# Four weight tiles worked through in halves at the start of a two-layer encoder trunk

## The chip, the core and the metric

The kernel runs on one NeuronCore of a Trainium2 chip. Time is what the device takes for one execution, in microseconds. Lower is better. Five engines have queues of their own that run in order: TensorE (PE, matmuls), VectorE (DVE), ScalarE (ACT), GpSimd (POOL) and SyncE (SP), which here issues every DMA. A semaphore ties one queue to another wherever one reads what the other writes.

## The reference, cut to what matters

Two layers, each with an input projection of the normalised sequence, two head groups (RWKV-7 scans in both directions, and windowed attention with a sink), gates, and an output projection onto the residual. What the change touches is the first projection of layer 0:

```python
for l in range(DEPTH):                       # DEPTH = 2, x is (1, 256, 2048) f32
    h = rms_norm(x, norm_g[l])
    proj = jnp.einsum('btd,dc->btc', h, w_in[l])
    rw_in, g_rw, q, k_at, v_at, g_at = jnp.split(proj, col_splits, axis=-1)
    rw_in = bidir_token_shift(rw_in, shift_mu[l])
    r, k, v, xw, xa = jnp.split(rw_in, rw_splits, axis=-1)
    ...
    x = x + jnp.einsum('btc,cd->btd', mix, w_out[l])
return rms_norm(x, final_g)
```

## The kernel before

The sequence lies transposed: 2048 channels are 16 rows of 128 partitions, and each row holds 256 positions. `X0[:, k, :]` is row k of the input, `xT` its place in memory. A weight tile gives 128 output columns; it has 16 rows of 128 × 128 and is loaded as two pieces of 8 rows (512 KB each) into buffers `raw`, of which there are three.

Single precision is kept by splitting. ScalarE rounds a weight piece to `hi` (L241) and VectorE makes `lo`, the rest (L243), each in two instructions of 4 rows; the input is split the same way into `XH` (L203) and `XL` (L204). A row of a tile is then three matmuls into one accumulator `pm`: `hi` by XH (L311), `hi` by XL (L312), `lo` by XH (L313). There are two buffers of hi and two of lo.

The queue of rows is the class `Stream`. `S.run(n)` issues n rows ("steps"); the split of the next piece is put into the program two rows before the present one ends; `S.later(n, fn)` puts `fn` n rows further on. `gemm` appends a tile as two pieces of 8 rows and, behind the last, its evacuation `evac`. TensorE's order is the order of the code; the other engines' orders are set by a scheduler, within what the data allow.

The tiles of layer 0 begin with tile 0 (xw) and tile 1 (xa), then four for each of eight head pairs: k, v, r and a gate. The first row of a k tile also calls `ups` (L509), which loads two small pieces for the pair, `iup` (96 partitions) and `dup` (97 partitions), into `g`.

The norm is applied after the projection, so the matmuls need not wait for it. ScalarE squares the input in four instructions of 1024 columns and VectorE adds them (tile `mv`, L256). `Norm.add` sums over partitions on TensorE (`pr`, L217), VectorE and GpSimd make the inverse root, `Norm.spread` puts it on all partitions with four matmuls (`pr<-dg`, L227), and ScalarE copies it to `rb` (L229). Every evacuation multiplies `pm` by `rb` (`u`, L453), so none can begin before. Behind the k tile's evacuation stands a chain to `sl`, which the matmuls `pk` (L706) need.

At the start all 16 rows of x are split with one step of tile 0 behind each, and then:

```python
S.later(20, lambda: L0.norm.add([ACC[:, i * T : (i + 1) * T] for i in range(4)]))
S.later(27, lambda: L0.norm.spread())
S.run(8)
```

Of the kernel before, what the change touches and what calls it, by code (L numbers as in the profile page):

```python
# [9 lines left out]
F32 = mybir.dt.float32  # L10
# [85 lines left out]
C_KEEP = C_OFF["band"]  # L96
# [37 lines left out]
def hybrid_trunk_kernel(ctx, tc, xT, wi, wv, wo, par, fing, dup, iup, sink, pos, cst, out):  # L134
# [21 lines left out]
    def wbank(name):  # L156
        return wpair(name)[:, 0]
# [73 lines left out]
    def wload(src):  # L231
        raw = wrp.tile([128, 1024], F32, tag="raw", name="raw")
        SY.dma_start(out=raw, in_=src)
        return raw

    def wsplit(raw):
        hi = wsp.tile([128, 1024], F32R, tag="hi", name="hi")
        lo = wsp.tile([128, 1024], F32R, tag="lo", name="lo")
        for i in range(2):
            q = slice(i * 512, (i + 1) * 512)  # L240
            A.activation(hi[:, q], raw[:, q], AF.Copy)  # L241
            with tc.high_priority(offset=PRIO_LO):
                V.tensor_tensor(lo[:, q], raw[:, q], hi[:, q].bitcast(F32), op=ALU.subtract)  # L243
        return hi, lo

    def halves(src, raws=None):
        return [lambda i=i: wsplit(raws[i] if raws else wload(src[i])) for i in range(2)]

    class InTurn:

# [43 lines left out]

    S = Stream()

    def gemm(src, operands, evac, raws=None, begin=None, bank=None):

        box = []

        def step(kk):
            def f(w):
                if not box:
                    box.append(bank() if bank else ps_main.tile([128, T], F32, tag="m", name="pm"))
                    if begin:
# [5 lines left out]
                PE.matmul(pm, wh, rh[:, kk, :], start=(kk == 0), stop=False)  # L311
                PE.matmul(pm, wh, rl[:, kk, :], start=False, stop=False)  # L312
                PE.matmul(pm, wl, rh[:, kk, :], start=False, stop=(kk == 15))  # L313

            return f

        ld = halves(src, raws)
        S.add(ld[0], [step(k) for k in range(8)])
        S.add(ld[1], [step(k) for k in range(8, 16)], lambda: evac(box[0]))

    first_w = [wrp.tile([128, 1024], F32, tag="raw", name="raw") for _ in range(2)]
    G0 = cp.tile([128, NKT], F32, name="G0")
    X0 = Rows("s0", F32, "X0")
    SY.dma_start(out=first_w[0][:, 0:512], in_=wi[0, 0, 0, :, 0:512])
    SY.dma_start(out=G0, in_=par[0, :, P_NG : P_NG + NKT])
    for a, b in ((0, 2), (2, 4), (4, 8), (8, 12), (12, 16)):
        SY.dma_start(out=X0[:, a:b, :], in_=xT[:, a:b, :])
        if a == 0:
            SY.dma_start(out=first_w[0][:, 512:1024], in_=wi[0, 0, 0, :, 512:1024])
        if a == 4:  # L330
            SY.dma_start(out=first_w[1], in_=wi[0, 0, 1])
    mhalf = cp.tile([128, 4], F32, name="mhalf")
    V.memset(mhalf, -0.5)

# [106 lines left out]
    def queue_inputs(l):  # L441
# [4 lines left out]
        def inproj(ct, evac, **kw):  # L446
            gemm(wi[l, ct], lambda: (L.XH, L.XL), evac, **kw)
# [49 lines left out]

        if l == 0:

            inproj(0, lambda pm: S.later(29, lambda: xw_evac(pm)), raws=first_w, bank=lambda: wbank("pm")[:, 0:T])  # L500
            inproj(1, lambda pm: S.later(13, lambda: xa_evac(pm)))
        else:
            inproj(0, xw_evac)
            inproj(1, xa_evac)
# [27 lines left out]
            return evac  # L532

        for p, t in enumerate(L.ts):
            inproj(2 + 4 * p, shift_evac(p, new(t, "k", "kr", 4)), begin=ups(p, t))
            inproj(3 + 4 * p, value_evac(p, t))
            inproj(4 + 4 * p, shift_evac(16 + p, new(t, "r", "kr", 4)))
            inproj(5 + 4 * p, silu_evac(new(t, "gr", "vg", 8)))

# [744 lines left out]
```

## Time and profile before

| | |
|---|---|
| median of 3 runs | 1176.88 us (1175.71 to 1177.16) |
| the profiled execution | 1176.53 us, span 1174.8 us |
| TensorE busy | 1148.4 us, 98% of the span |
| VectorE, ScalarE busy | 907.0 us, 781.6 us |
| mean granted TensorE clock | 0.994 |
| moved by DMA | 166.63 MB |

Times in the views are microseconds from the start of the span. A row of a timeline has its start, its length, the engine, the line, the operation, output<-inputs, the shapes and the count; in brackets stands how long the engine had been idle before, and what ended that. In a table of windows a row has the stretch and its length, then the busy time of PE, PEld, DVE, ACT and POOL with the number of instructions, then TensorE's granted clock, the share of the 16 DMA engines that was busy, and GB/s. SPq is SyncE's queue of DMA issues; its rows show the issue, not the transfer. The chain of waits goes back from the last instruction, at each step to what released it.

### The profile page before, as it was taken

To read this page: it belongs to the slowest core of one execution; us is meant where nothing else is said; L and a number is where in the kernel's file an instruction comes from. 1 tells how busy PE (TensorE), PEld (TensorE's weight loads), DVE (VectorE), ACT (ScalarE), POOL (GpSimd) and SP (SyncE) were. 2 spreads that over 40 slices of the span, in tenths; PEclk is the share of its full clock that TensorE was granted. 3 is DMA by queue.
4 is the path that set the end of the run, shared out by engine and by line. 5 is a ranking of instruction groups with operands and counts; after the bars stand their busy time and mean duration, and the time that the engine had idled before them with its cause. 6 is when DMAs were issued, how large, how long until landed. Compare 5 with 4: busy or idle time off the path is not lost.

```text
span 1174.8 us, 38087 instructions
## 1 busy us (share of the span) xinstructions
PE 1148.4 (98%) x16151; PEld 1073.7 (91%) x16151; DVE 907.0 (77%) x2017; ACT 781.6 (67%) x1971; POOL 21.7 (2%) x23
## 2 busy tenths in 40 slices
PE   8999999999999999999999999999999999999996
PEld 6998999899899999899999889999999999899996
DVE  6899978888877677766678888978887767786654
ACT  6667867776875666645556677876786666675553
POOL 0000000000000000000000000000000000000000
PEclk8999999999999999999999999999999999999998
DMA  7544333333333443477655443333233344346653
GB/s 258 168 152 133 119 111 119 107 98 117 109 112 124 129 126 120 133 244 233 213 176 176 139 134 115 109 107 127 97 112 110 120 132 126 105 143 193 213 190 124
DMA packets 60410, 166.63 MB, mean 142 GB/s; under 512 B 7728, under 2 KB 22736, under 8 KB 60240
## 3 DMA queue, kind: packets, MB, share of 16 engines
q1 hardware_dynamic: 60240, 164.21, 43.4%
q8 instruction: 126, 2.06, 0.7%
q14 instruction: 44, 0.36, 0.1%
HBM read 157.37 MB, written 4.19 MB: 138 GB/s over the span
## 4 chain that ended last, share of the span: by engine, by line
PE 63%; DVE 15%; issue 14%; ACT 5%; DMA 2%; SPq 0%; POOL 0%; DVEq 0%; POOLq 0%; ACTq 0%
PE pm L311 15%; PE pm L313 13%; PE pm L312 13%; DVE lo L243 4%; PE pg L832 3%; PE pcc L995 2%; DVE kd L256 1%; ACT hi L241 1%; PE py L1007 1%; DVE th L256 1%; PE py L980 1%; PE pcc L1023 1%; PE pd L939 1%; DVE FR L256 1%; DVE mv L256 1%
## 5 line engine op out<-in xcount | busy, mean ns | idle before, releaser
L243 DVE TENSOR_TENSOR lo<-raw,hi 128x512 fp32r<-128x512 f32 x560 | 372.2, 687 | 112.9 <-ACT hi L241 107.3
L241 ACT ACTIVATE hi<-raw 128x512 fp32r<-128x512 f32 x560 | 329.6, 625 | 168.0 <-PE pm L312 95.2
L311 PE MATMUL pm<-XHa,hi 128*128 128x256 f32 x832 | 246.9, 297 | 1.9 <-ACT XHa L203 1.4
L311 PE MATMUL pm<-XHb,hi 128*128 128x256 f32 x832 | 243.2, 292 | 0.0
L313 PE MATMUL pm<-XHb,lo 128*128 128x256 f32 x832 | 233.8, 281 | 2.4 <-DVE lo L243 2.4
L313 PE MATMUL pm<-XHa,lo 128*128 128x256 f32 x832 | 234.2, 281 | 1.3 <-DVE lo L243 1.1
L312 PE MATMUL pm<-XLa,hi 128*128 128x256 f32 x832 | 234.3, 282 | 0.5 <-DVE XLa L204 0.3
L312 PE MATMUL pm<-XLb,hi 128*128 128x256 f32 x832 | 233.7, 281 | 0.0
L311 PEld LDWEIGHTS pm<-XHa,hi 128*128 128x128 f32 x832 | 157.0, 189 | 14.9 <-issue 3.2
L311 PEld LDWEIGHTS pm<-XHb,hi 128*128 128x128 f32 x832 | 157.0, 189 | 5.5
L313 PEld LDWEIGHTS pm<-XHb,lo 128*128 128x128 f32 x832 | 157.0, 189 | 3.2 <-DVE lo L243 3.2
L313 PEld LDWEIGHTS pm<-XHa,lo 128*128 128x128 f32 x832 | 157.3, 189 | 2.5 <-DVE lo L243 2.5
L312 PEld LDWEIGHTS pm<-XLa,hi 128*128 128x128 f32 x832 | 157.4, 189 | 1.1 <-DVE XLa L204 1.1
L312 PEld LDWEIGHTS pm<-XLb,hi 128*128 128x128 f32 x832 | 157.1, 189 | 0.3 <-DVE XLb L204 0.3
L1018 ACT ACTIVATE suv<-pcc 64x128 f32<-64x128 f32 x128 | 34.5, 270 | 72.3 <-PE pcc L1016 48.7
L311 PE MATMUL pm<-MHa,hi 128*128 128x256 f32 x256 | 72.0, 281 | 0.0
L313 PE MATMUL pm<-MHa,lo 128*128 128x256 f32 x256 | 71.9, 281 | 0.0
L312 PE MATMUL pm<-MLb,hi 128*128 128x256 f32 x256 | 71.8, 280 | 0.0
L311 PE MATMUL pm<-MHb,hi 128*128 128x256 f32 x256 | 71.7, 280 | 0.0
L313 PE MATMUL pm<-MHb,lo 128*128 128x256 f32 x256 | 71.7, 280 | 0.0
L312 PE MATMUL pm<-MLa,hi 128*128 128x256 f32 x256 | 71.7, 280 | 0.0
L311 PEld LDWEIGHTS pm<-MHa,hi 128*128 128x128 f32 x256 | 48.2, 188 | 0.8 <-issue 0.8
(292 smaller groups left out, 2317.3 us busy)
## 6 DMA issues: line engine op xcount, KB each, us to landing
raw<-wi SPq DMA_DIRECT2D x207, 512.0 KB
raw<-wo SPq DMA_DIRECT2D x64, 512.0 KB
raw<-wv SPq DMA_DIRECT2D x8, 512.0 KB
rrot<-u SPq DMA_DIRECT2D x80, 32.0 KB
vg<-xT SPq DMA_DIRECT2D x16, 128.0 KB
xd<-vg SPq DMA_DIRECT2D x16, 128.0 KB
vg<-xd SPq DMA_DIRECT2D x16, 128.0 KB
g<-dup SPq DMA_DIRECT2D x16, 97.0 KB
```

The costliest lines, as they stand in the source:

```text
L241: A.activation(hi[:, q], raw[:, q], AF.Copy)
L243: V.tensor_tensor(lo[:, q], raw[:, q], hi[:, q].bitcast(F32), op=ALU.subtract)
L256: return lambda *a, **k: tc.keep_in_program_order(getattr(self.engine, name)(*a, **k))
L311: PE.matmul(pm, wh, rh[:, kk, :], start=(kk == 0), stop=False)
L312: PE.matmul(pm, wh, rl[:, kk, :], start=False, stop=False)
L313: PE.matmul(pm, wl, rh[:, kk, :], start=False, stop=(kk == 15))
L832: PE.matmul(pg[:, h, c * 128 : (c + 1) * 128], BK[half[h], d, c, 1 - h : 3 - h, :].rearrange("p s j -> p (s j)"), MV[half[h], d, c].rearra ...
L939: PE.matmul(narrow(pd[:, d], h, c), hx(TT, d, c, h), sub(QF, h ^ d, d, c, d * b), start=True, stop=True)
L980: PE.matmul(py[half[h], c, :], GE[h][:, d, c, 1, :], SUV[:, d, c, h, :], start=(i == 0 and d == 0), stop=(i >= NC // 2), skip_group_check= ...
L995: PE.matmul(pc[half[h], 0, d, :], GE[h][r, d, ci[d], 0, :], SUV[r, d, ci[d], h, :], start=True, stop=True)
L1007: PE.matmul(py[half[h], ci[d], :], MV[half[h], d, ci[d], 1, :], SUV[half[h], d, ci[d], h, :], start=False, stop=False, skip_group_check=True,)
L1018: A.activation(here(h), pc[half[h], 1], AF.Copy)
```

## The change

The first four tiles (0, 1, 2 and 3) go into a list first. Their four first halves are put into the stream, in that order, then their second halves in the order 2, 0, 1, 3. The first loads are whole pieces of 512 KB: the first half of tile 0, x rows 0 to 3 and 4 to 7, the first halves of tiles 1 and 2, x rows 8 to 11. The rows 12 to 15 of x are loaded further down in the code, behind 27 steps. The accumulators of tiles 0 and 1 share one pair of banks, and the delays of the evacuations and of the norm have new numbers: `Norm.spread` came after 43 steps and comes after 53.

```diff
-    first_w = [wrp.tile([128, 1024], F32, tag="raw", name="raw") for _ in range(2)]
+    first_w = [wrp.tile([128, 1024], F32, tag="raw", name="raw") for _ in range(3)]
...
-    SY.dma_start(out=first_w[0][:, 0:512], in_=wi[0, 0, 0, :, 0:512])
+    SY.dma_start(out=first_w[0], in_=wi[0, 0, 0])
     SY.dma_start(out=G0, in_=par[0, :, P_NG : P_NG + NKT])
-    for a, b in ((0, 2), (2, 4), (4, 8), (8, 12), (12, 16)):
+    for a, b in ((0, 4), (4, 8), (8, 12)):
         SY.dma_start(out=X0[:, a:b, :], in_=xT[:, a:b, :])
-        if a == 0:
-            SY.dma_start(out=first_w[0][:, 512:1024], in_=wi[0, 0, 0, :, 512:1024])
         if a == 4:
-            SY.dma_start(out=first_w[1], in_=wi[0, 0, 1])
+            for i in (1, 2):
+                SY.dma_start(out=first_w[i], in_=wi[0, i, 0])
...
-            inproj(0, lambda pm: S.later(29, lambda: xw_evac(pm)), raws=first_w, bank=lambda: wbank("pm")[:, 0:T])
-            inproj(1, lambda pm: S.later(13, lambda: xa_evac(pm)))
+            inproj(0, lambda pm: S.later(7, lambda: xw_evac(pm)), raws=first_w[0:1], bank=bank_of(0), queue=lead)
+            inproj(1, xa_evac, raws=first_w[1:2], bank=bank_of(1), queue=lead)
...
+            ke = shift_evac(p, new(t, "k", "kr", 4))
+            if l == 0 and p == 0:
+                inproj(2, lambda pm, ke=ke: S.later(14, lambda: ke(pm)), raws=first_w[2:3], begin=ups(p, t), queue=lead)
+                inproj(3, value_evac(p, t), queue=lead)
+                for x in [a for a, _ in lead] + [lead[i][1] for i in (2, 0, 1, 3)]:
+                    S.add(*x)
...
-    for k in range(NKT):
+    for k in range(8):
         x_split(L0.XH, L0.XL, X0[:, k, :], k, 0)
         S.run(1)
+    S.run(12)
+    for k in range(8, 12):
+        x_split(L0.XH, L0.XL, X0[:, k, :], k, 0)
+        S.run(1)
+    SY.dma_start(out=C, in_=cst[:, 0:C_KEEP])
+    setup_ = setup()
+    S.run(7)
+    SY.dma_start(out=X0[:, 12:16, :], in_=xT[:, 12:16, :])
+    SY.dma_start(out=PR, in_=par.rearrange("l p n -> p l n"))
+    for k in range(12, 16):
+        x_split(L0.XH, L0.XL, X0[:, k, :], k, 0)
...
-    S.later(20, lambda: L0.norm.add([ACC[:, i * T : (i + 1) * T] for i in range(4)]))
-    S.later(27, lambda: L0.norm.spread())
-    S.run(8)
-    SY.dma_start(out=C, in_=cst[:, 0:C_KEEP])
-    SY.dma_start(out=PR, in_=par.rearrange("l p n -> p l n"))
-    setup_ = setup()
+    S.later(15, lambda: L0.norm.add([ACC[:, i * T : (i + 1) * T] for i in range(4)]))
+    S.later(22, lambda: L0.norm.spread())
     next(setup_)
-    S.run(8)
+    S.run(1)
```

Three places in the engines' orders. The first is SP's queue of loads, before, from the last loads of x on; `raw_220` and `raw_266` are tile 1, `raw_317` is the first half of tile 2, `t1` is the positions, and `C`, `PR` and `cst` are constants:

```order
L327 DMA X0b_89<-xT 128x1024 x2
L233 DMA raw_220<-wi 128x1024
L233 DMA raw_266<-wi 128x1024
L1182 DMA C_84<-cst 128x642
L1183 DMA PR_83<-par 128x2x124
L349 DMA t1_282<-pos 128x256
L350 DMA FG_113<-fing 128x16
L351 DMA SK_114<-sink 128x32
L233 DMA raw_317<-wi 128x1024
L513 DMA g_335<-iup 96x2x128
L513 DMA g_337<-dup 97x2x128
L353 DMA mv_286<-cst 128x960
```

And after, from the third load of x on; `raw_246` is the first half of tile 3, `raw_282` the second half of tile 2, `raw_355` that of tile 0:

```order
L331 DMA X0b_90<-xT 128x1024
L527 DMA g_218<-iup 96x2x128
L527 DMA g_220<-dup 97x2x128
L233 DMA raw_246<-wi 128x1024
L1195 DMA C_84<-cst 128x642
L233 DMA raw_282<-wi 128x1024
L1198 DMA X0b_90<-xT 128x1024
L1199 DMA PR_83<-par 128x2x124
L352 DMA t1_314<-pos 128x256
L353 DMA FG_112<-fing 128x16
L354 DMA SK_113<-sink 128x32
L233 DMA raw_355<-wi 128x1024
```

`iup` and `dup` moved from behind the constants and tile 2 to the place behind x rows 8 to 11, and x rows 12 to 15 moved from ahead of them to the fourth place behind them.

The second is VectorE around the additions of the squares, before; `raw_266` is the second half of tile 1:

```order
L243 TENSOR_TENSOR lo_223<-raw_220,hi_222 128x512 x2
L256 TENSOR_TENSOR mv_236<-mv_236,mv_238 128x1024
L356 TENSOR_TENSOR DP_101<-PR_83 128x26
L359 TENSOR_SCALAR DP_101<-PR_83 128x8
L256 TENSOR_TENSOR mv_236<-mv_236,mv_241 128x1024
L243 TENSOR_TENSOR lo_269<-raw_266,hi_268 128x512 x2
L256 TENSOR_TENSOR mv_236<-mv_236,mv_244 128x1024
```

After, where `raw_355` is the second half of tile 0 and `raw_412` that of tile 1:

```order
L256 TENSOR_TENSOR mv_303<-mv_303,mv_305 128x1024
L256 TENSOR_TENSOR mv_303<-mv_303,mv_308 128x1024
L243 TENSOR_TENSOR lo_358<-raw_355,hi_357 128x512
L256 TENSOR_TENSOR mv_303<-mv_303,mv_311 128x1024
L243 TENSOR_TENSOR lo_358<-raw_355,hi_357 128x512
L243 TENSOR_TENSOR lo_415<-raw_412,hi_414 128x512 x2
```

The additions moved from the second half of tile 1 to the second half of tile 0, which is worked through third from last of the eight halves, and the last addition stands between the two `lo` of that piece.

The third is TensorE at the spread of the norm, before, in the second half of tile 2 (`pm_334`), 35 steps ahead of `pk`:

```order
L311 MATMUL pm_334<-XHb_132,hi_374 128x256
L312 MATMUL pm_334<-XLb_134,hi_374 128x256
L313 MATMUL pm_334<-XHb_132,lo_375 128x256
L227 MATMUL pr_351<-dg_353,C_84 128x128 x2
L311 MATMUL pm_334<-XHb_132,hi_374 128x256
```

After, in the second half of tile 1 (`hi_414`; `pm_142` is the pair of banks of tiles 0 and 1):

```order
L311 MATMUL pm_142<-XHb_131,hi_414 128x256
L312 MATMUL pm_142<-XLb_133,hi_414 128x256
L313 MATMUL pm_142<-XHb_131,lo_415 128x256
L227 MATMUL pr_397<-dg_399,C_84 128x128 x2
L311 MATMUL pm_142<-XHb_131,hi_414 128x256
```

`pk` kept its place behind 78 steps, so 25 steps now lie between the two.

More of the change, by code (lines that the diff above doesn't have):

```diff
@@ L246, in halves @@
     def halves(src, raws=None):
-        return [lambda i=i: wsplit(raws[i] if raws else wload(src[i])) for i in range(2)]
+        return [lambda i=i: wsplit(raws[i] if raws and i < len(raws) else wload(src[i])) for i in range(2)]
     class InTurn:
@@ L295, in hybrid_trunk_kernel, with gemm @@
     S = Stream()
-    def gemm(src, operands, evac, raws=None, begin=None, bank=None):
+    def gemm(src, operands, evac, raws=None, begin=None, bank=None, queue=None):
         box = []
@@ L317, in gemm @@
         ld = halves(src, raws)
-        S.add(ld[0], [step(k) for k in range(8)])
-        S.add(ld[1], [step(k) for k in range(8, 16)], lambda: evac(box[0]))
-    first_w = [wrp.tile([128, 1024], F32, tag="raw", name="raw") for _ in range(2)]
+        parts = (ld[0], [step(k) for k in range(8)]), (ld[1], [step(k) for k in range(8, 16)], lambda: evac(box[0]))
+        if queue is not None:
+            queue.append(parts)
+        else:
+            for x in parts:
+                S.add(*x)
+    first_w = [wrp.tile([128, 1024], F32, tag="raw", name="raw") for _ in range(3)]
     G0 = cp.tile([128, NKT], F32, name="G0")
     X0 = Rows("s0", F32, "X0")
-    SY.dma_start(out=first_w[0][:, 0:512], in_=wi[0, 0, 0, :, 0:512])
+    SY.dma_start(out=first_w[0], in_=wi[0, 0, 0])
     SY.dma_start(out=G0, in_=par[0, :, P_NG : P_NG + NKT])
-    for a, b in ((0, 2), (2, 4), (4, 8), (8, 12), (12, 16)):
+    for a, b in ((0, 4), (4, 8), (8, 12)):
         SY.dma_start(out=X0[:, a:b, :], in_=xT[:, a:b, :])
-        if a == 0:
-            SY.dma_start(out=first_w[0][:, 512:1024], in_=wi[0, 0, 0, :, 512:1024])
         if a == 4:
-            SY.dma_start(out=first_w[1], in_=wi[0, 0, 1])
+            for i in (1, 2):
+                SY.dma_start(out=first_w[i], in_=wi[0, i, 0])
     mhalf = cp.tile([128, 4], F32, name="mhalf")
@@ L498, in queue_inputs, with bank_of, bank @@
         if l == 0:
-            inproj(0, lambda pm: S.later(29, lambda: xw_evac(pm)), raws=first_w, bank=lambda: wbank("pm")[:, 0:T])
-            inproj(1, lambda pm: S.later(13, lambda: xa_evac(pm)))
+            lead = []
+            pair = []
+            def bank_of(i):
+                def bank():
+                    if not pair:
+                        pair.append(wpair("pm"))
+                    return pair[0][:, i, 0:T]
+                return bank
+            inproj(0, lambda pm: S.later(7, lambda: xw_evac(pm)), raws=first_w[0:1], bank=bank_of(0), queue=lead)
+            inproj(1, xa_evac, raws=first_w[1:2], bank=bank_of(1), queue=lead)
         else:
@@ L534, in queue_inputs @@
         for p, t in enumerate(L.ts):
-            inproj(2 + 4 * p, shift_evac(p, new(t, "k", "kr", 4)), begin=ups(p, t))
-            inproj(3 + 4 * p, value_evac(p, t))
+            ke = shift_evac(p, new(t, "k", "kr", 4))
[3 more added lines that the diff above has]
+                for x in [a for a, _ in lead] + [lead[i][1] for i in (2, 0, 1, 3)]:
+                    S.add(*x)
+            else:
+                inproj(2 + 4 * p, ke, begin=ups(p, t))
+                inproj(3 + 4 * p, value_evac(p, t))
             inproj(4 + 4 * p, shift_evac(16 + p, new(t, "r", "kr", 4)))
```

## The prediction

> **What bounds the kernel now.** I read the page first, for the engine that carries the span.
>
> ```profile
> span 1174.8 us, 38087 instructions
> ...
> PE 1148.4 (98%) x16151; PEld 1073.7 (91%) x16151; DVE 907.0 (77%) x2017; ACT 781.6 (67%) x1971; POOL 21.7 (2%) x23
> ...
> PE 63%; DVE 15%; issue 14%; ACT 5%; DMA 2%; SPq 0%; POOL 0%; DVEq 0%; POOLq 0%; ACTq 0%
> ```
>
> TensorE is idle for 26.4 us in all, so a change to the start can give a few us at most. The profiled execution took 1176.53 us, 1.7 more than its span and 0.35 under the median of 1176.88. What a measurement can tell from no change, 0.2%, is 2.35 us. Next come TensorE's timeline and its granted clock over the start.
>
> ```profile
> 6.64 0.38 PE L311 MATMUL pm<-XHa,hi 128*128 128x256 f32 x1 [0.57 <-ACT XHa L203]
> 22.47 0.38 PE L313 MATMUL pm<-XHb,lo 128*128 128x256 f32 x1 [1.22 <-DVE lo L243]
> 26.60 1.84 PE L217 MATMUL pr<-C,mv 128*128 128x1 f32 x16
> 28.30 0.36 PE L311 MATMUL pm<-XHa,hi 128*128 128x256 f32 x1
> 33.84 0.28 PE L311 MATMUL pm<-XHa,hi 128*128 128x256 f32 x1
> 39.47 0.28 PE L311 MATMUL pm<-XHa,hi 128*128 128x256 f32 x1
> ```
> ```profile
> 5.92:9.33 3.41, 2.22 (x11) 1.47 (x11) 2.36 (x5) 2.34 (x5) 0.00 (x0) 1.00 0.97 299
> 9.33:12.75 3.41, 2.63 (x11) 2.10 (x11) 1.83 (x5) 2.41 (x6) 0.00 (x0) 0.50 1.02 410
> 12.75:16.16 3.41, 3.41 (x16) 3.13 (x16) 3.41 (x8) 3.41 (x9) 0.00 (x0) 0.50 1.01 366
> 19.57:22.99 3.41, 2.20 (x18) 1.99 (x18) 3.41 (x7) 3.35 (x8) 0.00 (x0) 1.00 0.08 28
> ```
>
> I count in steps: one row of a weight tile, three matmuls. Tile 3 begins at 33.84 and tile 4, step 64, at 39.47, so a step takes 0.352 us. From step 64 on TensorE's order is the same in both programs; 39.47 is the mark to beat. The norm's sums (26.60 to 28.30) cost 1.7 us. In the second table the third pair is TensorE's busy time, and the column of 1.00 and 0.50 its clock: half speed from 9.33 to 16.16.
>
> **Where the transfers are.** The DMA queue of SP hands eight semaphores round, so each issue below waited for the transfer eight places ahead of it, and its start dates that landing.
>
> ```profile
> 10.34 0.34 SPq L349 DMA_DIRECT2D t<-pos  x1
> 11.58 0.33 SPq L350 DMA_DIRECT2D FG<-fing  x1
> 12.86 0.33 SPq L351 DMA_DIRECT2D SK<-sink  x1
> 14.46 0.33 SPq L233 DMA_DIRECT2D raw<-wi  x1
> 15.67 0.33 SPq L513 DMA_DIRECT2D g<-iup  x1
> 16.93 0.27 SPq L513 DMA_DIRECT2D g<-dup  x1
> ```
>
> They date X0[4:8], the second weight piece, X0[8:12], X0[12:16] and the two pieces behind: about 1.25 us per 512 KB, and 3,080 KB landed by 14.46. Then something odd:
>
> ```profile
> 20.90:23.10 2.20, 0.98 (x8) 0.78 (x8) 2.20 (x4) 2.13 (x6) 0.00 (x0) 1.00 0.07 22
> ```
> ```profile
> 27.19 0.96 DVE L365 CAST LV<-mv 128x1536 uint8<-128x1536 f32 x1 [1.11 <-DMA mv<-cst]
> ```
> ```profile
> 59.19 5.48 DMA raw<-wi
> ```
>
> For 2 us the 16 DMA engines move 22 GB/s at a share of 0.07, one engine of 16. What is under way is `dup`, the last load issued before (16.93): 97 KB, all on one engine. At 22 GB/s it streams for 4.5 us. What stands behind it on that engine is late: `cst`, issued at 21.84, was only there at 27.19, and in the chain of waits a later 512 KB piece behind the next `dup` takes 5.48 us.
>
> **The change, part by part.**
>
> *First pieces.* X0[0:4] and the whole first weight piece must land before the first matmul (1,032 KB, where 520 KB do now), so TensorE starts about 1.5 us later than 6.64, near 8. Rows 4 to 7 need 1,544 KB as before: 10.34. The clock falls as before, and by 16.16 TensorE has done about 12 steps in either program. Nothing gained or lost there.
>
> *`iup` and `dup` overtake.* They stood behind 5.2 MB; now they stand behind X0[8:12], 3.1 MB, and the loads of tile 3's first half, C, tile 2's second half, X0[12:16], PR and tile 0's second half stand behind them. Six pieces and G0 are ahead: 3,080 KB, 14.4 by the rows above. `iup` (96 KB) is spread: 0.2. `dup`: at least 4.5 by its rate; at most 6.1, since `cst` less its 480 KB (1.17) starts at 26.0 while the 1,205 KB from C to `iup` end no earlier than 16.93 + 2.9. I take 5.0, near the rate, as the small loads in that stretch are slow too. Then 512, 321, 512 and 512 KB: 4.5. X0[12:16] lands at 14.4 + 0.2 + 5.0 + 4.5 = 24.1 instead of 14.46.
>
> Tile 3's first half lands near 20.9, and TensorE wants it at 16.16 + 12 × 0.352 = 20.4: with hi and lo a stall of 1.5 to 2. It costs nothing in the end, since the next wait is longer.
>
> *The squares.* Their order on ScalarE and VectorE:
>
> ```profile
> 12.99 3.29 ACT L203 ACTIVATE XHb<-X0b,G 128x256 fp32r<-128x256 f32 x8
> 16.19 1.14 ACT L241 ACTIVATE hi<-raw 128x512 fp32r<-128x512 f32 x2
> 17.23 2.00 ACT L256 ACTIVATE mv<-X0a 128x1024 f32<-128x1024 f32 x2
> 20.07 0.62 ACT L241 ACTIVATE hi<-raw 128x512 fp32r<-128x512 f32 x1
> 20.59 1.05 ACT L256 ACTIVATE mv<-X0b 128x1024 f32<-128x1024 f32 x1
> ```
> ```profile
> 21.73 1.28 DVE L243 TENSOR_TENSOR lo<-raw,hi 128x512 fp32r<-128x512 f32 x2
> 22.93 1.22 DVE L256 TENSOR_TENSOR mv<-mv 128x1024 f32<-128x1024 f32 x1
> ```
>
> Four XHb take 3.29 / 2 = 1.65, so the first square starts at 25.8, 8.6 later than now (17.23). The same chain then gives the first lo of tile 0's second half at 21.73 + 8.6 = 30.3 and its matmul, the stalled one at 22.47, at 31.0. TensorE wanted it at step 40, near 27.9: idle 3 us. The third addition now stands between the two lo (1.2), so the second is done at 30.3 + 0.6 + 1.2 + 0.7 = 32.8, and 46 steps are done at 33.2. The sums take 1.7 (34.9), the 18 steps left 6.3, the spread of the norm (four matmuls) 0.4: step 64 at 41.6, against 39.47. **+2.2 us.** Tile 0's second half itself lands by 27.3 at the latest and is hidden by the squares with 1.3 to spare.
>
> *Norm later, first use where it was.* The spread moves from step 43 to step 53, the matmuls `pk` stay at step 78.
>
> ```profile
> 31.64 0.61 PE L227 MATMUL pr<-dg,C 128*128 128x128 f32 x4
> 32.00 0.36 PE L311 MATMUL pm<-XHb,hi 128*128 128x256 f32 x1
> 44.52 0.28 PE L706 MATMUL pk<-sl,BONES 128*128 128x256 f32 x1
> ```
> ```profile
> 32.85 0.74 DVE L453 TENSOR_TENSOR u<-pm,rb 128x256 f32<-128x256 f32 x2
> ...
> 42.16 0.42 DVE L256 TENSOR_TENSOR sl<-t,mf 128x256 fp32r<-128x256 f32 x1
> ```
>
> VectorE needs 9.7 us from u to sl (32.85 to 42.58) and is done 1.9 before `pk`. The new queue has one lo less and one shift more there: 9.5. With 0.7 from the spread to u that is 10.2 after it, and TensorE arrives after 25 steps, 8.9. **+1.2 us** (bounds: 0, if waits inside the 9.7 vanish, and 2).
>
> Behind that all queues agree again; the later stalls stay. Sum: +3.4 us, 1179.9 on the profiled execution, 1180.3 on the median.
>
> **The rivals.**
>
> *The first transfers run faster.* 256 KB landed by 3.33, 520 KB by 6.08, 1,544 KB by 10.34:
>
> ```profile
> 3.33 0.63 ACT L241 ACTIVATE hi<-raw 128x512 fp32r<-128x512 f32 x1 [1.32 <-DMA raw<-wi]
> 6.08 0.51 ACT L203 ACTIVATE XHa<-X0a,G 128x256 fp32r<-128x256 f32 x1 [2.12 <-DMA X0a<-xT]
> 10.34 0.91 ACT L203 ACTIVATE XHa<-X0a,G 128x256 fp32r<-128x256 f32 x2 [1.79 <-DMA X0a<-xT]
> ```
>
> At the later 1.25 per 512 KB the last two stretches would take 0.6 and 2.5, not 2.75 and 4.26: 3.9 earlier. If larger pieces bring that, all moves up by 3.9: -1.7 + 1.2 = -0.5, 1176.4. Against it: X0[4:8], a whole 512 KB piece, was slow too, so time rather than size seems to matter. 14%. The Trainium skill, DMA: Bandwidth & Descriptors, section Bandwidth, speaks for this case: it asks for batches of 1 MiB or more; no run here isolates the size.
>
> *`dup` holds nothing up.* Then X0[12:16] lands at 19.1 and TensorE runs from step 12 at 16.16 through 34 steps to 28.1, with sums, spread and 18 steps to 36.5: -2.9. With the wait at `pk` 1175.2 (14%). If VectorE also reaches sl in time, 1174.0, **faster** (13%). The point that decides is X0[12:16] landing before about 19.5; against it speaks the late `cst`.
>
> *The clock falls a second time.* At 9.33 it fell after a window 65% busy in which no idle stretch exceeded 0.6 us, at 22.99 it did not after one as busy. The wait of 3 us at step 40 leaves its windows about half busy. Half clock over one or two windows of 3.41 loses 1.5 or 3.0: 1181.8 to 1183.3, 12%. The Trainium skill, TensorE: Matmul & The Clock Gate, section Why this matters for your kernels, puts the danger at idle gaps over about 3 us; the fall at 9.33, with no such gap, shows this case can be touchier.
>
> *The change is not what it says.* Its code says all four first halves first, and TensorE's order follows it. But the fourth half and X0[12:16] are not among the first loads.
>
> **How the numbers follow.** The forecast has 47%: 1178.5 to 1182. About 39 of it and the 12 of the clock lie above 1179.2 (slower 0.51), 8 and the rivals at 1175.2 and 1176.4 within (same 0.36), 13 below 1174.5. The range reaches from 1174.0 to 1183.0; the forecast's own is 1178.5 to 1182.
>
> **What would show it.** Right: a stretch at 22 GB/s near 15 to 19, waits of TensorE on lo of 1.5 us or more near 21 and of 3 near 28, one on sl of about 1, tile 4 starting after 41. Wrong: X0[12:16] split before 20, tile 4 before 38, or no wait at `pk`.

## The result, and the profile after

The changed kernel takes 1180.77 us (median of 6 runs, 1179.04 to 1183.81) against 1176.26 us for the kernel before, measured beside it (1175.36 to 1177.16): a ratio of 1.0042, 95% interval 1.0027 to 1.0056. Measured again on another chip it was 1179.16 against 1176.90 us, ratio 1.0019 (1.0010 to 1.0027). It is slower, by 2.2 to 4.9 us as the two ratios give it. The profiled execution took 1180.64 us, the span 1178.9.

TensorE's timeline first: its first step, the waits, the sums, the spread, step 64 and `pk`.

```profile
9.52 0.58 PE L311 MATMUL pm<-XHa,hi 128*128 128x256 f32 x1 [3.42 <-ACT XHa L203]
...
26.98 0.38 PE L311 MATMUL pm<-XHb,hi 128*128 128x256 f32 x1 [1.06 <-ACT hi L241]
29.12 0.38 PE L313 MATMUL pm<-XHb,lo 128*128 128x256 f32 x1 [1.64 <-DVE lo L243]
31.45 1.84 PE L217 MATMUL pr<-C,mv 128*128 128x1 f32 x16
36.91 0.95 PE L227 MATMUL pr<-dg,C 128*128 128x128 f32 x4
39.13 0.39 PE L311 MATMUL pm<-XHb,hi 128*128 128x256 f32 x1 [0.91 <-DVE u L456]
42.80 0.28 PE L311 MATMUL pm<-XHa,hi 128*128 128x256 f32 x1
...
47.91 0.34 PE L727 MATMUL pk<-sl,BONES 128*128 128x256 f32 x1
```

The sums come at 31.45 (26.60 before), step 64 at 42.80 (39.47) and `pk` at 47.91 (44.52): 3.39 us late, and no wait stands at `pk`. VectorE shows how close that was: `sl` ends at 47.81, 0.1 before `pk` starts, and `u`, which needs the norm's `rb`, starts 5.5 us later than the 32.85 of before.

```profile
38.32 0.76 DVE L456 TENSOR_TENSOR u<-pm,rb 128x256 f32<-128x256 f32 x2 [1.08 <-ACT rb L229]
47.40 0.41 DVE L256 TENSOR_TENSOR sl<-t,mf 128x256 fp32r<-128x256 f32 x1
```

Next SyncE's queue. Each row is an issue; its length is how long SyncE was busy with it.

```profile
5.84 0.37 SPq L527 DMA_DIRECT2D g<-dup  x1
6.33 7.13 SPq L233 DMA_DIRECT2D raw<-wi  x1
13.51 0.43 SPq L1195 DMA_DIRECT2D C<-cst  x1
14.13 0.33 SPq L233 DMA_DIRECT2D raw<-wi  x1
14.50 0.43 SPq L1198 DMA_DIRECT2D X0b<-xT  x1
14.98 0.45 SPq L1199 DMA_DIRECT2D PR<-par  x1
```

The piece behind `dup` holds SyncE for 7.13 us, where such an issue otherwise takes 0.33. With so little issued, the 16 DMA engines, which move 406 GB/s from 10 to 11 us, move 89 from 12 to 13 and 44 from 13 to 14. X0[12:16], which stands behind 31 steps in the code (8, 12, 4 and 7; not 27, as said above), is issued at 14.50, and ScalarE and VectorE date its landing and that of PR by waiting for them, though not for long (0.42 and 0.80 us):

```profile
21.80 1.71 ACT L203 ACTIVATE XHb<-X0b,G 128x256 fp32r<-128x256 f32 x4 [0.42 <-DMA X0b<-xT]
23.42 1.99 ACT L256 ACTIVATE mv<-X0a 128x1024 f32<-128x1024 f32 x2
```
```profile
23.63 0.19 DVE L359 TENSOR_TENSOR DP<-PR 128x26 f32<-128x26 f32 x1 [0.80 <-DMA PR<-par]
```

Last the clock, in windows (after the busy times comes the clock, as 1.00 or 0.50):

```profile
27.39:30.80 3.41, 1.77 (x13) 1.47 (x12) 3.41 (x5) 2.40 (x4) 0.00 (x0) 1.00 0.37 106
30.80:34.22 3.42, 3.36 (x29) 3.36 (x30) 2.11 (x5) 0.19 (x1) 0.66 (x1) 1.00 0.73 222
34.22:37.63 3.41, 3.41 (x20) 3.41 (x18) 2.42 (x9) 0.96 (x2) 0.69 (x1) 0.50 0.36 133
300.46:303.87 3.41, 1.63 (x45) 1.29 (x43) 2.79 (x7) 3.35 (x12) 0.00 (x0) 1.00 0.44 136
303.87:307.28 3.41, 3.41 (x17) 3.41 (x17) 3.04 (x8) 3.40 (x9) 0.00 (x0) 0.50 0.07 23
```

It falls at 34.22. The window just ahead of that has TensorE busy for 3.36 us, about half of it with the norm's sums; the window with the waits is the one before. It falls again at 303.87, behind a TensorE wait of 1.78 us on ScalarE that the kernel before has too (1.76 us at 299.46, without a fall in its one profile; its other executions may have one). Read at the first `pk` of each head pair, the lag is 3.2 to 3.5 us until 261 us, 4.7 behind the fall at 304, and 4.1 to 4.2 at the end. So of the span's 4.1 us the start gave some 3.2, and a fall of the clock far from the change the rest.

### The profile page after: what moved, and what is told of

Read it like the earlier page. It is cut to its first block, busy times and chain, and to the rows that moved or that the text cites. A ratio compares the mean times of both kernels' runs of the same rounds, so it can differ in the third digit from the quotient of the medians.

```text
span 1178.9 us, 38079 instructions
## 1 busy us (share of the span) xinstructions
PE 1150.1 (98%) x16151; PEld 1076.4 (91%) x16151; DVE 906.9 (77%) x2017; ACT 781.3 (66%) x1971; POOL 22.3 (2%) x23
## 4 chain that ended last, share of the span: by engine, by line
PE 67%; DVE 15%; issue 14%; ACT 3%; DMA 1%; SPq 0%; POOL 0%; DVEq 0%; POOLq 0%; ACTq 0%
PE pm L311 17%; PE pm L313 14%; PE pm L312 14%; DVE lo L243 4%; PE pg L853 3%; PE pcc L1016 2%; PE py L1028 1%; DVE kd L256 1%; PE pcc L1044 1%; DVE th L256 1%; DVE mv L256 1%; PE py L1001 1%; PE pd L960 1%; PE pcc L1034 1%; PE pza L712 1%
```

## The experiments

Times below are medians, with the ratio to the kernel before on the same chip and its 95% interval; the ratio is taken from all the runs and need not be the quotient of the two medians. Of each kernel there is one profile, of the changed one there are two. The table gathers the marks of the start from the profiles; landings are those of the trace's completion records.

| kernel | first step | X0[8:12], X0[12:16] landed | sums | u | sl done | pk | ratio |
|---|---|---|---|---|---|---|---|
| before | 6.64 | 12.8, 14.4 | 26.60 | 32.85 | 42.58 | 44.52 | 1 |
| changed | 9.52 | 14.4, 21.8 | 31.45 | 38.32 | 47.81 | 47.91 | 1.0042 |
| changed, again | 8.43 | 13.2, 20.8 | 31.33 | 37.35 | 46.85 | 46.90 | 1.0019 |
| dup in two | 9.39 | 14.5, 19.6 | 32.10 | 37.81 | 47.29 | 47.39 | 1.0008 |
| later evacuation | 8.85 | 13.7, 20.9 | 31.49 | 37.20 | 46.65 | 46.70 | 1.0028 |
| both | 7.45 | 13.3, 18.5 | 28.51 | 34.22 | 43.66 | 43.71 | 1.0009 |
| before + overtaking | 6.75 | 12.5, 16.9 | 28.93 | 34.47 | 44.55 | 46.53 | 1.0021 |
| small first pieces | 6.05 | 13.1, 22.3 | 33.00 | 38.71 | 48.19 | 48.25 | 1.0046 |
| early squares | 9.18 | 13.7, 15.1 | 27.41 | 37.67 | 44.84 | 47.87 | 1.0025 |
| early squares, dup in two | 8.43 | 13.1, 14.9 | 27.76 | 37.01 | 44.20 | 47.33 | 1.0038 |
| fill | 9.05 | 13.5, 20.9 | 31.81 | 41.09 | 50.58 | 50.64 | 1.0026 |
| own bank | 8.23 | 12.9, 15.6 | 28.87 | 35.35 | 44.41 | 44.47 | 1.0023 |
| own bank, dup whole | 7.54 | 12.2, 14.8 | 27.44 | 33.94 | 43.01 | 43.07 | 1.0010 |
| dup behind | 9.09 | 13.5, 16.0 | 26.98 | 36.21 | 46.17 | 46.22 | 1.0030 |

### dup in two transfers

```diff
+                    if n == "du" and l == 0 and p == 0:
+                        for a, b in ((0, RANK), (RANK, rows)):
+                            SY.dma_start(out=t[n][a:b], in_=src[l, :, a:b, p * 128 : (p + 1) * 128].rearrange("d r c -> r d c"))
+                        continue
                     SY.dma_start(out=t[n][0:rows], in_=src[l, :, :, p * 128 : (p + 1) * 128].rearrange("d r c -> r d c"))
```

RANK is 96. 

> The changed kernel, with the first pair's 97 rows of dup loaded in two transfers, of 96 rows and of one row, so that the rows are no longer all on one DMA engine. Theory A (the late sums are the price of the overtaking: dup on one engine holds SyncE's issue of tile 3's piece for 7.13 us, and with it C, tile 2's second piece, X0[12:16] and PR): SyncE's issue behind dup takes under 1 us, X0[12:16] lands at 18 to 20 us in place of 21.8 and PR at 19 to 21 in place of 23.6, TensorE's 2.7 us of waits at step 40 shrink to under 1, step 64 starts 1.5 to 3 us sooner than 42.80, and the time is 1177.8 to 1179.5, 1 to 3 us under the changed kernel. Rival B (the order of the halves itself costs: two more split tiles, the squares' order on ScalarE and VectorE, the bank pair that tiles 0 and 1 share): the loads come sooner, but step 64 stays within 0.7 us of 42.80, and the time within 0.7 us of 1180.8. Rival C (the clock's second fall at 34 us does it): the time follows whether a window at half clock stands between 20 and 45 us, and not the loads: 1178.5 to 1179.3 without one, whatever the loads do.

1177.35 us, ratio 1.0008 (0.9999 to 1.0018). On time and loads theory A came true, on TensorE's waits rival B did: those at step 40 add up to 1.68 us, and step 64 starts at 42.28, only 0.52 sooner. The 96 rows landed at 15.1, 0.3 behind `iup` (whole: 16.7 in the changed kernel, 2.1 behind it). The piece behind is issued in 0.37, and the DMA engines move 311 and 326 GB/s in the two microseconds from 12 to 14. X0[12:16] is issued hardly sooner than the 14.50 of the changed kernel, since SyncE waits ahead of it until VectorE's `lo` frees a weight buffer:

```profile
14.38 0.43 SPq L1202 DMA_DIRECT2D X0b<-xT  x1
```

It lands 5.1 us after X0[8:12] where it took 7.3 and 7.6, because the pieces ahead of it had landed sooner. But the sums came no sooner: 22.7 us after TensorE's first step, against 21.9 and 22.9. ScalarE's timeline says why:

```profile
20.69 1.15 ACT L241 ACTIVATE hi<-raw 128x512 fp32r<-128x512 f32 x2 [0.91 <-PE pm L312]
21.75 1.70 ACT L203 ACTIVATE XHb<-X0b,G 128x256 fp32r<-128x256 f32 x4
```

X0[12:16] lay there from 19.6, but its splits stand behind a `hi` that waits until TensorE gives a buffer back. With the loads in time, that wait stands where the transfer stood. So the times fell by more than this profile can account for, and rival C is not excluded. The profiled run took 1179.08 us and has a fall of the clock at 28.59. It is one of four runs of 1179.08 to 1179.99 us with a mean granted clock of 0.992; the other seven have 0.995 to 0.997 and took 1176.45 to 1177.47.

The Trainium skill, DMA: Bandwidth & Descriptors, section Why a DMA increments its semaphore by 16 and not by 1, has a transfer run on the largest number of engines up to 16 that divides its row count, so 96 rows on 16 and 97, a prime number, on one. The runs agree, with 22 GB/s for 97 rows before and 0.3 us behind `iup` for 96.

### Tile 0's evacuation two steps later

```diff
-            inproj(0, lambda pm: S.later(7, lambda: xw_evac(pm)), ...
+            inproj(0, lambda pm: S.later(9, lambda: xw_evac(pm)), ...
```

> The changed kernel, with the evacuation of tile 0 (which needs the norm's row factors) put in two steps later in program order, behind the last step of tile 1, so that step 54's matmul doesn't wait until VectorE has read the bank pair that tiles 0 and 1 share (0.91 us at 39.13). Theory A (that wait only stands where the wait for the norm at pk would stand otherwise: VectorE takes 9.5 us from u to sl either way): the wait at 39.13 goes, step 64 starts 0.9 us sooner, and TensorE waits 0.9 us at pk instead; the time is within 0.4 us of the changed kernel. Rival B (the bank pair's wait is a loss of its own): 0.7 to 1.1 us under the changed kernel.

1179.57 us, ratio 1.0028 (1.0016 to 1.0040). The wait at the bank (0.91 us, and 1.29 in the second profile of the changed kernel) went and came back at `pk`, larger, as theory A had it. The time cannot tell the two apart, since the ratio lies between the two measurements of the changed kernel:

```profile
46.70 0.39 PE L727 MATMUL pk<-sl,BONES 128*128 128x256 f32 x1 [1.41 <-DVE sl L256]
```

### Both edits

> The changed kernel with both edits: dup of the first pair in two transfers, and tile 0's evacuation two steps later. Theory A: with the loads in time the sums end early, so that neither the bank pair nor pk holds TensorE for more than 0.5 us: 1177.0 to 1178.7, and against the kernel with dup's edit alone -0.9 to +0.2. Rival B (the halves cost of themselves): within 0.7 us of the changed kernel; rival C (what is left is the norm's chain on VectorE, 9.5 us from u to sl against ten steps of 3.5 us and the work between): as theory A in the loads, but with a wait at pk of 1 us or more and no difference from the kernel with dup's edit alone.

1177.88 us, ratio 1.0009 (1.0000 to 1.0018): no difference from dup's edit alone, as rival C had it, with

```profile
43.71 0.38 PE L731 MATMUL pk<-sl,BONES 128*128 128x256 f32 x1 [1.31 <-DVE sl L256]
```

Two kernels thus show one thing: in the changed order `pk` is set by VectorE's chain from `u` (9.4 to 9.5 us in both, as in the profiles of the changed kernel), and what TensorE saves ahead of it is given back there. The profile of this kernel has `pk` 0.8 us sooner than before, and is 2 us behind at the end: about 1.5 us were lost at a fall of the clock at 299, and some 1.4 more between 500 and 620 us, which no fall on record explains. TensorE's early start, at 7.45, is part of the early `pk`.

### The overtaking alone, in the kernel before

```diff
         SY.dma_start(out=X0[:, a:b, :], in_=xT[:, a:b, :])
+        if a == 8:
+            for n, src, rows in (("iu", iup, RANK), ("du", dup, RANK + 1)):
+                first_u[n] = st("g", [2, 128], bufs=2)
+                SY.dma_start(out=first_u[n][0:rows], in_=src[0, :, :, 0:128].rearrange("d r c -> r d c"))
```

> The kernel before, and of the change the overtaking alone: iup and dup of the first pair are issued behind X0[8:12] and ahead of tile 0's second half and all that follows. Theory A (dup on one engine holds SyncE for some 7 us and with it tile 0's second half or tile 1's first and X0[12:16]): TensorE, which has a row ready each 0.7 us, waits 2 to 5 us around steps 8 to 14, and the norm is late by as much: 2.5 to 5 us over before (1178.8 to 1181.3). Rival B (dup's overtaking is harmless, and the halves' order costs the 4.5 us): within 0.6 us of before, with X0[12:16] landing within 1.5 us of 14.46.

1179.45 us, ratio 1.0021 (1.0012 to 1.0030): 1.4 to 3.5 us, in theory A's place, near its lower end. (In this kernel tile 0's second half is issued ahead of X0[8:12], so it is not among the loads that `dup` holds up; X0[12:16] is the first of them.) SyncE's row and TensorE's, then the windows, in which a clock of 0.98 or 0.52 means that the window lies across the edge of a stretch at half clock:

```profile
6.12 6.32 SPq L328 DMA_DIRECT2D X0b<-xT  x1
```
```profile
17.47 0.38 PE L311 MATMUL pm<-XHb,hi 128*128 128x256 f32 x1 [2.13 <-ACT XHb L203]
```
```profile
15.88:19.29 3.41, 1.69 (x10) 1.49 (x11) 1.81 (x5) 2.38 (x6) 0.00 (x0) 0.98 1.01 392
19.29:22.70 3.41, 3.41 (x18) 3.41 (x18) 2.29 (x3) 3.41 (x5) 0.00 (x0) 0.52 0.83 288
```

Here nothing of the halves is in the kernel, so the overtaking has a price by itself: X0[12:16] at 16.9 in place of 14.4, a wait of 2.13 us, and a stretch at half clock behind it. Whether `dup` in two would take that price away in this order was not run.

### The changed kernel again, and the small first pieces

> The changed kernel itself, on the chip of the three kernels that are run with it. 1179.5 to 1181.5 us, 2.5 to 4.5 over before on this chip, if the first measurement holds here; its runs scatter over some 4 us. Theory: they scatter because X0[0:4] lands late by as much as 2 us and because the clock falls to one half for one more stretch of 3.4 us in some runs; then the slowest runs have the lowest mean clock.

1179.16 us (1177.37 to 1180.81), 2.3 over before: less than in the first measurement, and just under the expected 1179.5. The eight runs with a mean clock of 0.992 or 0.993 took 1178.60 to 1180.81 us, the three with 0.994 or 0.995 took 1177.37 to 1179.03, as the theory had it. The sums again came at 31.33, with waits at step 40 of 0.40 and 1.22 where the first profile had 1.06 and 1.64. The clock fell for one stretch at 28, none at 304. X0[12:16] landed at 20.8, while ScalarE was still at a `hi` that had waited for TensorE, so its splits did not wait for it:

```profile
20.20 1.15 ACT L241 ACTIVATE hi<-raw 128x512 fp32r<-128x512 f32 x2 [0.75 <-PE pm L312]
21.26 1.70 ACT L203 ACTIVATE XHb<-X0b,G 128x256 fp32r<-128x256 f32 x4
```

The small first pieces:

```diff
-    SY.dma_start(out=first_w[0], in_=wi[0, 0, 0])
+    SY.dma_start(out=first_w[0][:, 0:512], in_=wi[0, 0, 0, :, 0:512])
...
-    for a, b in ((0, 4), (4, 8), (8, 12)):
+    for a, b in ((0, 2), (2, 4), (4, 8), (8, 12)):
         SY.dma_start(out=X0[:, a:b, :], in_=xT[:, a:b, :])
+        if a == 0:
+            SY.dma_start(out=first_w[0][:, 512:1024], in_=wi[0, 0, 0, :, 512:1024])
```

> The changed kernel with the first pieces as they were before: tile 0's first half in two loads of 256 KB, and X0[0:4] in two of two rows. Theory A (the prediction's: TensorE starts 1.5 us or more sooner, but works through those steps at half clock or waits, so that the same step is reached at the time of the sums): TensorE's first step at 6.6 to 7.0 us in place of 9.5, and the time within 0.7 us of the changed kernel. Rival B (the larger pieces are a loss of their own, since TensorE starts 2.9 us later and never waits long enough afterwards to make it up): 1.5 to 2.9 us under the changed kernel.

1183.41 us, ratio 1.0046 (1.0031 to 1.0061): rival B fell, and theory A erred on the other side.

```profile
6.05 0.39 PE L311 MATMUL pm<-XHa,hi 128*128 128x256 f32 x1 [0.20 <-ACT XHa L203]
...
19.73 0.39 PE L311 MATMUL pm<-XHa,hi 128*128 128x256 f32 x1 [1.41 <-ACT hi L241]
...
28.11 0.39 PE L311 MATMUL pm<-XHb,hi 128*128 128x256 f32 x1 [1.87 <-ACT hi L241]
```

TensorE starts 2.4 us sooner than in the kernel beside it and is 1.7 later at step 40: two more transfers stand ahead of `dup`, the issue behind `dup` is held until 14.7 us (13.5 in the first profile), and X0[12:16] lands 1.5 later. An early first matmul buys nothing here, with `dup` whole. The runs fall into two groups, four from 1179.35 to 1180.46 us and five from 1183.41 to 1185.57 with a lower mean clock (0.992 to 0.994, and 0.987 to 0.991); the profile is of the first group.

### The norm's work moved forward

The squares go between the steps, one by one, the sums to step 35, the spread to 46, the evacuation to 51; X0[12:16] is issued behind X0[8:12]. Of two kernels the second has dup in two as well.

```diff
-    for a, b in ((0, 4), (4, 8), (8, 12)):
+    for a, b in ((0, 4), (4, 8), (8, 12), (12, 16)):
...
-    S.later(15, lambda: L0.norm.add([ACC[:, i * T : (i + 1) * T] for i in range(4)]))
-    S.later(22, lambda: L0.norm.spread())
+    S.later(8, lambda: L0.norm.add([ACC[:, i * T : (i + 1) * T] for i in range(4)]))
+    S.later(19, lambda: L0.norm.spread())
```

> The changed kernel with the norm's work moved forward and dup left whole: X0[12:16] issued right behind X0[8:12], the four squares put on ScalarE one by one between the splits of the weight halves, the sums at step 35, the spread at step 46, and tile 0's evacuation at step 51. Theory A (what makes TensorE wait 1.6 to 2.7 us at step 40 and 0.9 to 1.4 at the bank pair or at pk is the place of the squares and of the norm in the engines' program order: on ScalarE they stand behind splits that wait until TensorE gives a hi tile back, whatever the loads do): no wait over 0.5 us at step 40 nor at pk, and the time 2.5 to 4.5 us under the changed kernel, 1176 to 1178. Rival B (the held loads are the cause: raw pieces behind dup still land late): 0 to 1 us under the changed kernel, with a wait of 1 us or more on a weight half.

> The same early norm, and the first pair's dup in transfers of 96 rows and of one. Theory A: the two edits add up: dup's edit gave about 2 us where the sums came late, but with X0[12:16] ahead of it only the weight pieces are behind dup, and TensorE needs the first of them at step 24: 0 to 1 us under the kernel with the early norm alone, 1174.5 to 1177, and under before. Rival B (dup still holds back what TensorE waits for): 2 us or more under the kernel with the early norm alone. Rival C (another wait takes the place of those removed, on VectorE's chain from u to sl of 9.5 us): within 0.7 us of the kernel with dup's edit alone, 1177 to 1178.

1180.67 us, ratio 1.0025 (1.0015 to 1.0034), and 1181.97 us, 1.0038 (1.0026 to 1.0051): both expectations fell. The sums came 4 us sooner (27.4 and 27.8), yet `pk` only at 47.9 and 47.3, 3.0 and 3.1 us after `sl` was done: now TensorE was late itself. In the second kernel:

```profile
20.97 0.38 PE L311 MATMUL pm<-XHa,hi 128*128 128x256 f32 x1 [1.99 <-ACT hi L241]
22.66 0.58 PE L313 MATMUL pm<-XHa,lo 128*128 128x256 f32 x1 [1.19 <-DVE lo L243]
```

Tile 3's first half had landed behind X0[12:16], `iup`, `dup` and C (17.7 us; with `dup` whole 20.6), and its split stood behind the squares. There are two chains to `pk`, and I had moved one by holding up the other.

### Filling the wait at step 40

```diff
+    def fill():
+        L0.norm.ps = wpair("pr")
+        for _ in range(6):
+            PE.matmul(L0.norm.ps[:, 1, T : 2 * T], L0.XH[:, 0, 0:128], L0.XH[:, 0, :], start=True, stop=True)
+
+    S.later(9, fill)
     S.later(15, lambda: L0.norm.add(
```

> The changed kernel with six more 128x256 matmuls, whose result nobody reads, ahead of the first step of tile 0's second half, where TensorE waits for the half's hi and lo (0.40 and 1.22 us in the last profile of the changed kernel, 1.06 and 1.64 in the first). Theory A (the wait is what makes the clock fall a second time, for one stretch of 3.4 us at half, which costs 1.2 to 1.7 us): no granted clock of one half between 20 and 45 us, and 0.5 to 1.5 us under the changed kernel, so a ratio to before of about 1.001. Rival B (the clock falls for the 16 one-column matmuls or for the waits before): the fall stays and the time is within 0.4 us of the changed kernel. Rival C (what sets pk is VectorE's chain behind the norm, not TensorE): the fall goes, TensorE reaches pk sooner and waits there for sl, and the time is within 0.4 us.

1178.96 us, ratio 1.0026 (1.0011 to 1.0040): no gain, so theory A is not borne out, and the fall of the clock stayed, as rival B had it. The fill ran ahead of the first wait only; in the profile, the slowest run (1185.22), the wait for `lo` was 2.03 us, and then:

```profile
27.02:30.43 3.41, 1.38 (x11) 1.38 (x11) 3.31 (x5) 2.62 (x4) 0.00 (x0) 0.96 0.29 79
30.43:33.84 3.41, 3.41 (x19) 3.41 (x17) 1.51 (x3) 0.00 (x0) 0.00 (x0) 0.50 0.82 253
33.84:37.26 3.42, 3.42 (x17) 3.42 (x18) 1.41 (x4) 0.73 (x2) 1.34 (x1) 0.50 0.35 131
37.26:40.67 3.41, 3.41 (x19) 3.41 (x19) 1.90 (x7) 0.42 (x1) 0.00 (x0) 0.54 0.16 34
```

Three stretches at half clock, though TensorE never idles in them, and `pk` at 50.64, 2.7 and 3.7 later than in the two profiles of the changed kernel. The sums lie in this time (3.41 us in place of 1.84); whether their one-column matmuls count as work for the clock was not tried. That the changed kernel's clock fell at 34.22, right behind a window half filled by the sums, points the same way. It is the clearest case of how far two executions of nearly the same order can lie apart.

### Both chains moved

Tile 3's first half, X0[12:16], C and PR are issued right behind X0[8:12], dup in two behind them; the squares stand after steps 11, 15, 24 and 30, the sums at 45, the spread at 52; tile 0 has a bank of its own.

```diff
+        if k == 0:
+            late_w.append(wload(wi[0, 3, 0]))
+            SY.dma_start(out=X0[:, 12:16, :], in_=xT[:, 12:16, :])
+            SY.dma_start(out=C, in_=cst[:, 0:C_KEEP])
+            SY.dma_start(out=PR, in_=par.rearrange("l p n -> p l n"))
...
+            own = (lambda: ps_c.tile([128, 512], F32, tag="y", name="pm")[:, 0:T], lambda: wbank("pm")[:, 0:T])
```

> The changed kernel rearranged where the runs so far showed waits: tile 3's first half, X0[12:16], C and PR issued in that order right behind X0[8:12] and ahead of iup and dup (dup in two), the squares put on ScalarE after steps 11, 15, 24 and 30, the sums at step 45 and the spread at 52, tile 0 in a bank of its own and evacuated at step 52. Theory A (two chains end at pk, TensorE's own and the norm's through u and sl on VectorE, and only moving both moves pk): no wait over 0.6 us at steps 24, 32, 40 and at the bank, sums by 26.5, u by 31.5, pk at 40 to 42.5 us (44.52 before), and 1173 to 1175.5 us. Rival B (every order of the halves meets ScalarE's and VectorE's limit, since the splits of x and of four tiles and the squares all come in the first 25 us): a wait of 1 to 2 us at another half, pk at 44 or later, and 1176.5 to 1179.

> The same with dup in one transfer. Theory A (dup's price depends on what is issued behind it: here tile 2's second half, needed at step 32): that piece lands 1.5 to 3 us later, TensorE waits 0.5 to 2 us at step 32, and the time is 0.5 to 2 us over the kernel with dup in two. Rival B (dup's rows on one engine hold nothing up that TensorE waits for): within 0.4 us of it.

1179.69 us, ratio 1.0023 (1.0014 to 1.0032), and with dup whole 1178.65 us, 1.0010 (1.0001 to 1.0020). In the profiles `pk` came at 44.47 and 43.07, 0.05 and 1.45 us ahead of before, so the lateness at `pk` is gone, short of the 40 to 42.5 expected (waits of 0.8 to 1.2 us on a `lo` or a `hi` remain, rival B's picture). The end of both is 2.1 and 2.8 us behind before all the same: the clock fell at 301 and 302, and at 73 in the second, at about 1.5 us each time. On dup's price theory A fell: the piece behind it landed at 21.2 in place of 19.5, TensorE waited 0.81 us for it, and the time is no longer than with `dup` in two.

### dup behind everything

```diff
-                inproj(2, lambda pm, ke=ke: S.later(14, lambda: ke(pm)), raws=first_w[2:3], begin=ups(p, t), queue=lead)
+                inproj(2, lambda pm, ke=ke: S.later(14, lambda: ke(pm)), raws=first_w[2:3], queue=lead)
+                L.first_ups = ups(p, t)
...
+    S.later(9, L0.first_ups)
```

Besides, sums, spread and evacuation stand one or two steps earlier. 

> The rearranged kernel (early squares, tile 0 in its own bank) with iup and dup of the first pair, whole, issued at step 40, behind all weight pieces up to tile 0's second half, the sums at step 43, the spread at 50 and tile 0's evacuation at 51. Theory A (what the halves cost is the late norm and the pieces held by dup, and both go away here): X0[12:16] lands by 15.8 us, no wait over 0.6 us at steps 24, 32 and 40, sums by 26.5, u by 33, and pk at 41.5 to 43.5 us, 1 to 3 us under before's 44.52; the time is 1174 to 1176.5 where the clock doesn't fall a second time, some 1.6 us more where it does, so a median of 1175 to 1177.5 and a ratio to before of 0.9985 to 1.0005. Rival B (the halves are bound elsewhere, at the splits on ScalarE and VectorE): pk at 44 or later, 1178 to 1180, ratio 1.001 to 1.0025.

1180.95 us, ratio 1.0030 (1.0019 to 1.0041). Up to the sums things went nearly as theory A had it (X0[12:16] at 16.0 and the sums at 26.98, for 15.8 and 26.5; a wait of 0.78 at step 32), but `pk` came at 46.22, which is rival B's place, and the time is above both ranges. The rows of SyncE, ScalarE and TensorE:

```profile
23.00 0.34 SPq L520 DMA_DIRECT2D g<-dup  x1
23.38 5.24 SPq L233 DMA_DIRECT2D raw<-wi  x3
```
```profile
32.27 2.38 ACT L241 ACTIVATE hi<-raw 128x512 fp32r<-128x512 f32 x4 [7.48 <-DMA raw<-wi]
```
```profile
32.96 0.58 PE L311 MATMUL pm<-XHb,hi 128*128 128x256 f32 x1 [2.26 <-ACT hi L241]
```
```profile
32.87:36.28 3.41, 3.32 (x14) 3.10 (x15) 2.97 (x7) 2.09 (x5) 0.00 (x0) 0.51 0.37 112
```

The price of `dup` moved with it: the next weight half lands 8.8 us after its issue began, TensorE waits 2.26 us for it at step 48, and the clock falls. No version beat the kernel before.

## Why the prediction was right

The forecast was 1180.3 us, the ratio of 1.0042 gives 1181.8 on the median shown before it, and the second measurement 1179.1. Of the signs named for being right, tile 4 after 41 came (42.80 and 41.78), and the wait near 28 (2.70 us, and 1.62 in the second profile, of 3). The stall near 21 and the wait on `sl` did not come, the DMA engines were slow sooner and less (44 GB/s at 13 to 14 us), and a sign named for being wrong, no wait at `pk`, came true. So direction and size came out, and the path to them only in part.

*First pieces.* TensorE started at 9.52 and 8.43, 1.8 to 2.9 late where 1.5 was taken. That it costs nothing held with `dup` whole: the small pieces, with a start at 6.05, were no faster, but TensorE then waited 1.41 us at step 24 for the piece behind `dup`. Small pieces together with `dup` in two were not run. The small pieces also answer the rival of faster first transfers: in pieces of 256 KB X0[0:4] was there by 7.5 us, in one of 512 KB by 7.8 in the kernel beside it, and by 6.8 to 8.9 in all profiles. The Trainium skill (DMA: Bandwidth & Descriptors, section Bandwidth) asks for batches of 1 MiB or more; no run here has one, and the step from 256 to 512 KB brought nothing.

*`iup` and `dup` overtake.* The loads came late as forecast, but by less, and little hung on it. `dup` was done 2.1 us after `iup`, not 5.0; what let it overlap with the loads ahead wasn't tried. That SyncE itself would be held was not foreseen. X0[12:16] landed at 21.8 and 20.8, not 24.1, and tile 3's first half at 17.8 and 17.4, not 20.9, so TensorE had no stall there. In the first profile ScalarE waited 0.42 us for X0[12:16] and VectorE 0.80 for PR; in the second neither waited, and its waits at step 40 (1.62 us) are those of the kernel with `dup` in two (1.68). So the late loads, on which the forecast rested, account for about 1.1 us in one profile and for nothing in the other.

*The squares.* The first square started at 23.42 and 22.86 (25.8 forecast), and 46 steps were done at 31.45 and 31.33 (33.2). The idle at step 40 was 2.70 us in the first profile and 1.62 in the second, forecast 3. What was missed is that ScalarE's order alone keeps some 1.6 us there: the splits and squares stand behind a `hi` that waits for TensorE, and the waits are 1.68 and 1.55 us in the two kernels whose loads came sooner. The kernel before has as much:

```profile
30.71 0.38 PE L313 MATMUL pm<-XHb,lo 128*128 128x256 f32 x1 [0.52 <-DVE lo L243]
```

This wait and the 1.22 us at 22.47 make 1.74.

*From there to step 64.* Forecast 8.4 us, measured 11.35 and 10.45. The bank pair took 0.91 and 1.29, which the forecast lacked, and the half clock about 1.5 by estimate (in the changed kernel's profile matmuls follow each other in 0.118 us at full clock and in 0.213 in the stretch from 34.22, where the first profile lost it; the second lost it at 28, ahead of the sums). The clock's second fall was a rival at 12%; it happened in both profiles. Against the kernel before, step 64 is 3.33 and 2.31 us late. Of this about 1.5 is the clock's, 0.9 and 1.3 the bank's, and +1.0 and -0.1 the waits at step 40 over the 1.74 of before; 0.7 goes off, since step 16 came sooner (17.31 and 17.27, against 17.98), and 0.6 and 0.4 stay unexplained. So the +2.2 that the squares were to cost is not what happened; the half clock took its place. By luck the sum came out the same: `pk` is 3.39 late (2.38 in the second profile), +3.4 forecast.

*Wait at `pk`.* None stood there; the bank's wait took its place, since `u` released both. From `u` to the end of `sl` 9.5 us were forecast and 9.5 measured, and with the later evacuation the wait at `pk` is 1.41 (+1.2 forecast). The term's place was wrong, its cause and its size right.

*`dup` holds nothing up.* Its point of decision, X0[12:16] landing before 19.5, was reached with both edits (18.5) and nearly with dup in two alone (19.6). The times were then 1177.9 and 1177.4, not 1174.0 to 1175.2: in time the loads do not set TensorE free, since ScalarE's part stays.

What stays open: how much of the 2.2 to 4.9 us is dup's. In the order before its overtaking costs 1.4 to 3.5. In the changed order the two kernels with dup in two are 1.3 us or more faster on average, but this goes with the clock: among the runs with a mean clock of 0.992 the average is 1179.4 us in the changed kernel (second measurement, seven runs) and 1179.6 and 1179.4 with dup in two (four and five). With dup in two, seven and six of eleven runs have 0.995 or more, without it one of eleven. Whether the sooner loads keep the clock up is not shown, and in the two rearranged orders dup in two was no faster than dup whole.

## What to carry to other kernels

When work that all later work waits for (here the norm's row factors) is moved back, look for the chain behind it and its slack: 1.9 us were there, 5 were used. One edit on one of two chains that end together moves the wait and not the time. And a load with an awkward number of rows delays those that are issued behind it, wherever it is put. Cut in 96 rows and one it no longer did; whether that saves time depends on what waits for those loads.

## What the runs showed of the hardware

- In all nine profiles where another load follows it at once, the issue behind the 97-row load holds SyncE for 4.3 to 7.2 us (7.13, 6.32 and 7.21 in three of them), whether that issue is a weight piece, rows of x or C, and every load behind it waits. In two transfers, of 96 rows and one, it takes 0.36 or 0.37.
- Later than 15 us, the clock falls for stretches of 3.41 us at half speed right behind windows of that length in which TensorE was busy for at most 1.8 us, though no wait was over 2.3. The fall at 34.22 in the changed kernel is the one exception (3.36 us busy, half of it the sums). It is no firm rule: in the kernel before, a window with 1.66 us busy, ending at 299.47, has no fall behind it.
- Near 300 us all fourteen profiles have the same TensorE wait of about 1.8 us, and the clock fell behind it in seven, at about 1.5 us each time. In those seven the wait lies in one window (1.60 to 1.66 us busy), in six others it is split between two (1.86 or more in each); the kernel before is the exception. The two falls of the changed kernel, at 34.22 and 303.87, lie 269.65 us apart, 79 times 3.413. The Trainium skill, TensorE: Matmul & The Clock Gate, section What's actually happening, has a window of 3413 ns that runs free of the kernel's start; the lengths agree, and so does it that the same wait costs clock in one execution and not in another. Its rule of gaps over about 3 us (section Why this matters for your kernels) is too mild for these waits.
